# Layer normalisation without affine: two-pass statistics shared by three engines, rows normalised on GpSimd

## The chip, the cores and the metric

One NeuronCore of a Trainium2 chip runs the kernel. The metric is device time in microseconds (us), the median of several executions; the profile gives a span that is 1.7 to 2.5 us shorter. Engines are named as in the profile: DVE is VectorE, ACT is ScalarE, POOL is GpSimd, SP issues DMAs; ACTq and SPq are the instruction queues of ACT and SP. Where an instruction works on 8 or 1024 elements, that is per partition.

## The reference

```python
x = np.random.randn(32, 512, 1024).astype(np.float32)      # eps = 1e-5
mean = np.mean(x, axis=-1, keepdims=True)
var = np.var(x, axis=-1, keepdims=True)
return ((x - mean) / np.sqrt(var + eps)).astype(np.float32)
```

There are 16384 rows of 1024 numbers. A tile of K takes K rows on each of 128 partitions, so the whole is 128 rows a partition. 67.1 MB are read and 67.1 MB written.

## The kernel before

A ring of 48 rows a partition in SBUF holds six tiles of 8 rows. SP issues the loads, ACT the stores. DVE takes batch-norm statistics of each half row; ten small POOL operations make the mean and the squared sum of 8 rows at a time; ACT takes the root and normalises in place.

```python
TILES = (2, 2, 4) + (8,) * 14 + (4, 2, 2)
...
        for k in range(G):
            for s in range(NSUB):                       # NSUB = 2 halves of 512
                nc.vector.bn_stats(out=stats[:, k, s, :],
                                   in_=xs[:, k, s * BN_MAX : (s + 1) * BN_MAX])
...                                                     # ten small GpSimd operations: nmean, ss, nmr
        nc.scalar.activation(out=std[:, :G], in_=ss[:, :G], func=AF.Sqrt, bias=eps_t, scale=1.0 / D)
        nc.vector.reciprocal(out=rstd[:, :G], in_=std[:, :G])
...
        for k in range(G):
            nc.scalar.activation(out=xs[:, k, :], in_=xs[:, k, :], func=AF.Identity,
                                 bias=nmr[:, k : k + 1], scale=rstd[:, k : k + 1])
...
        for K, row, pos in place(TILES, RING):
            nc.sync.dma_start(out=ring[:, pos : pos + K, :], in_=rows_of(x2, row, K))
            group(...)
            nc.scalar.dma_start(out=rows_of(o2, row, K), in_=ring[:, pos : pos + K, :])
```

Of the kernel before, what the change touches and what calls it, by code (L numbers as in the profile page):

```python
# [1 line left out]

# [4 lines left out]


TILES = (2, 2, 4) + (8,) * 14 + (4, 2, 2)  # L10

RING = 48

GROUP = 8


def place(tiles, ring):

    plan, row, pos = [], 0, 0
    for K in tiles:  # L20
        if pos + K > ring:
            pos = 0
        plan.append((K, row, pos))
        row += K
        pos += K
    return plan


@with_exitstack
def kernel(  # L30
    ctx: ExitStack,
    tc: tile.TileContext,
    x: bass.AP,
    eps: bass.AP,
    out: bass.AP,
):
    nc = tc.nc
    P = nc.NUM_PARTITIONS
    eps_val = float(eps) if not isinstance(eps, bass.AP) else 1e-5

    x2 = x.flatten_outer_dims()
    o2 = out.flatten_outer_dims()
    N, D = x2.shape
    BN_MAX = nc.vector.BN_STATS_FMAX
    NSUB = D // BN_MAX
    assert sum(TILES) * P == N

    rings = ctx.enter_context(tc.tile_pool(name="rings", bufs=1))
    st = ctx.enter_context(tc.tile_pool(name="st", bufs=4))

    fdt = mybir.dt.float32
    AF = mybir.ActivationFunctionType
    ALU = mybir.AluOpType

    ring = rings.tile([P, RING, D], fdt)
    eps_t = rings.tile([P, 1], fdt)

    def rows_of(a, row, K):
        return a[row * P : (row + K) * P].rearrange("(p k) d -> p k d", p=P)

    def pool_sum(o, terms):
        G = terms.shape[1]
        half = st.tile([P, GROUP, 2], fdt, name="half")
        nc.gpsimd.tensor_tensor(  # L64
            out=half[:, :G], in0=terms[:, :, 0:2], in1=terms[:, :, 2:4], op=ALU.add
        )
        nc.gpsimd.tensor_tensor(  # L67
            out=o, in0=half[:, :G, 0], in1=half[:, :G, 1], op=ALU.add
        )

    def group(xs, G):
        stats = st.tile([P, GROUP, NSUB, 6], fdt, name="stats")
        for k in range(G):
            for s in range(NSUB):
                nc.vector.bn_stats(  # L75
                    out=stats[:, k, s, :],
                    in_=xs[:, k, s * BN_MAX : (s + 1) * BN_MAX],
                )

        H = 2 * NSUB  # L80
        parts = stats[:, :G].rearrange("p g s (h c) -> p g (s h) c", h=2)
        mean4, m2 = parts[:, :, :, 1], parts[:, :, :, 2]
        nmean = st.tile([P, GROUP], fdt, name="nmean")
        dev = st.tile([P, GROUP, H], fdt, name="dev")
        ss = st.tile([P, GROUP], fdt, name="ss")
        pool_sum(nmean[:, :G], mean4)
        nc.gpsimd.tensor_scalar(  # L87
            out=nmean[:, :G], in0=nmean[:, :G], scalar1=-1.0 / H, scalar2=None, op0=ALU.mult
        )
        nc.gpsimd.tensor_tensor(  # L90
            out=dev[:, :G],
            in0=mean4,
            in1=nmean[:, :G].unsqueeze(2).to_broadcast([P, G, H]),
            op=ALU.add,
        )
        nc.gpsimd.tensor_mul(out=dev[:, :G], in0=dev[:, :G], in1=dev[:, :G])  # L96
        nc.gpsimd.tensor_scalar(  # L97
            out=dev[:, :G], in0=dev[:, :G], scalar1=float(D // H), scalar2=None, op0=ALU.mult
        )
        nc.gpsimd.tensor_tensor(out=dev[:, :G], in0=dev[:, :G], in1=m2, op=ALU.add)  # L100
        pool_sum(ss[:, :G], dev[:, :G])
        std = st.tile([P, GROUP], fdt, name="std")
        nc.scalar.activation(  # L103
            out=std[:, :G], in_=ss[:, :G], func=AF.Sqrt, bias=eps_t, scale=1.0 / D
        )
        rstd = st.tile([P, GROUP], fdt, name="rstd")
        nc.vector.reciprocal(out=rstd[:, :G], in_=std[:, :G])  # L107
        nmr = st.tile([P, GROUP], fdt, name="nmr")
        nc.gpsimd.tensor_mul(out=nmr[:, :G], in0=nmean[:, :G], in1=rstd[:, :G])  # L109
        for k in range(G):  # L110
            nc.scalar.activation(  # L111
                out=xs[:, k, :],
                in_=xs[:, k, :],
                func=AF.Identity,
                bias=nmr[:, k : k + 1],
                scale=rstd[:, k : k + 1],
            )

    with tc.manual_schedule():
        nc.vector.memset(eps_t, eps_val)  # L120
        for K, row, pos in place(TILES, RING):
            nc.sync.dma_start(out=ring[:, pos : pos + K, :], in_=rows_of(x2, row, K))
            for g in range(0, K, GROUP):
                G = min(GROUP, K - g)
                group(ring[:, pos + g : pos + g + G, :], G)
            nc.scalar.dma_start(out=rows_of(o2, row, K), in_=ring[:, pos : pos + K, :])


# [1 line left out]
_INS = ['x', 'eps']  # L130
_OUTS = [((32, 512, 1024), 'float32')]

_NUMBERS = {'eps': 1e-05}


# [26 lines left out]
```

## Time and profile before

| | before |
|---|---|
| median time | 317.98 us (317.94 to 317.99) |
| span of the profile | 316.1 us |
| DVE, ACT, POOL busy | 157.1, 154.3, 45.1 us |
| load and store queue | 49.6% and 49.3% of 16 DMA engines |
| from one tile's statistics to the next | 19.4 us |

The two queues add up to 98.9% of what the DMA engines can do, and no engine is busy for more than half of the span. The lines that carry this stand in the prediction.

### The profile page before, as it was taken

The page shows a single profiled execution, that of the slowest core. Times are in us where ns is not written, and L with a number is a line of the kernel's source. Part 1 is how long each engine was busy: PE and PEld are TensorE (multiplying, and loading weights), DVE is VectorE, ACT ScalarE, POOL GpSimd, SP SyncE. Part 2 cuts the span into 40 slices and gives each one's busy share as a digit, 9 for nine tenths or more (in the row PEclk, how much of TensorE's full clock was granted, in tenths as well). Part 3 has the DMA queues.
Part 4 walks back from the last instruction along what each step waited for, and adds up shares of the span by engine and source line. Part 5 has one row for each costly group of instructions (what it writes and reads, how often), then busy time and mean ns, then how long its engine had stood idle before and what let it go on. Part 6 is the DMA issues. An engine that isn't in the chain of part 4 may idle for free.

```text
span 316.1 us, 794 instructions
## 1 busy us (share of the span) xinstructions
DVE 157.1 (50%) x277; ACT 154.3 (49%) x149; POOL 45.1 (14%) x204
## 2 busy tenths in 40 slices
DVE  2368596547092561916529074190652908363030
ACT  1336296692833809247091561900651956196321
POOL 0420202201102020020200202002020020221120
DMA  7999999999999999999999999999999999999996
GB/s 301 433 399 469 431 416 425 433 427 444 420 448 419 444 419 444 435 427 444 419 448 415 448 424 440 423 448 419 444 423 440 423 435 429 446 428 417 455 411 282
DMA packets 5766, 134.27 MB, mean 425 GB/s; under 512 B 640, under 2 KB 640, under 8 KB 640
## 3 DMA queue, kind: packets, MB, share of 16 engines
q1 hardware_dynamic: 2880, 67.11, 49.6%
q10 hardware_dynamic: 2880, 67.11, 49.3%
q14 instruction: 6, 0.05, 0.0%
HBM read 67.11 MB, written 67.11 MB: 425 GB/s over the span
## 4 chain that ended last, share of the span: by engine, by line
DMA 58%; DVE 17%; ACT 9%; POOL 6%; issue 3%; another core or an unknown queue 3%; ACTq 0%; POOLq 0%; DVEq 0%; SPq 0%
DMA ring<-in_x_dram 32%; DMA out_dram<-ring 27%; DVE stats L75 17%; ACT ring L111 8%; POOL half L64 1%; ACT std L103 1%; POOL dev L97 1%; POOL nmean L87 1%; POOL dev L100 1%; POOL dev L90 1%; POOL dev L96 1%; POOL nmean L67 1%; POOL ss L67 1%; DVE rstd L107 0%
## 5 line engine op out<-in xcount | busy, mean ns | idle before, releaser
L75 DVE BATCH_NORM_STATS2 stats<-ring 128x6 f32<-128x512 f32 x256 | 153.7, 678 | 71.2 <-DMA ring<-in_x_dram 71.2
L111 ACT ACTIVATE ring<-ring,nmr,rstd 128x1024 f32<-128x1024 f32 x128 | 147.0, 1227 | 10.8 <-POOL nmr L109 10.8
L103 ACT ACTIVATE std<-ss,eps_t 128x8 f32<-128x8 f32 (+2 forms) x20 | 6.0, 300 | 143.0 <-POOL ss L67 115.8
L107 DVE RECIPROCAL rstd<-std 128x8 f32<-128x8 f32 (+2 forms) x20 | 3.9, 193 | 77.3 <-ACT std L103 77.3
L64 POOL TENSOR_TENSOR half<-stats 128x16 f32<-128x16 f32 (+2 forms) x20 | 4.5, 226 | 221.0 <-DVE stats L75 221.0
L109 POOL TENSOR_TENSOR nmr<-nmean,rstd 128x8 f32<-128x8 f32 (+2 forms) x20 | 4.0, 202 | 27.2 <-DVE rstd L107 27.2
L97 POOL TENSOR_SCALAR dev<-dev 128x32 f32<-128x32 f32 (+2 forms) x20 | 5.6, 281 | 1.8
L100 POOL TENSOR_TENSOR dev<-dev,stats 128x32 f32<-128x32 f32 (+2 forms) x20 | 4.9, 243 | 1.7
L90 POOL TENSOR_TENSOR dev<-stats,nmean 128x32 f32<-128x32 f32 (+2 forms) x20 | 4.6, 231 | 1.7
L87 POOL TENSOR_SCALAR nmean<-nmean 128x8 f32<-128x8 f32 (+2 forms) x20 | 4.6, 228 | 1.8
L96 POOL TENSOR_TENSOR dev<-dev 128x32 f32<-128x32 f32 (+2 forms) x20 | 4.6, 228 | 1.6
L64 POOL TENSOR_TENSOR half<-dev 128x16 f32<-128x16 f32 (+2 forms) x20 | 4.2, 210 | 1.6
L67 POOL TENSOR_TENSOR nmean<-half 128x8 f32<-128x8 f32 (+2 forms) x20 | 4.0, 199 | 1.6
L67 POOL TENSOR_TENSOR ss<-half 128x8 f32<-128x8 f32 (+2 forms) x20 | 4.0, 199 | 1.6
L103 ACT ACT_TABLE_LOAD x1 | 1.3, 1283 | 0.9 <-DVE eps_t L120 0.9
L120 DVE MEMSET eps_t<- 128x1 f32 x1 | 0.1, 59 | 0.8 <-PEq L143 0.8
L143 POOL MEMSET const-float32-0.0<- 128x1 f32 x1 | 0.1, 98 | 0.2 <-issue 0.2
L143 POOL MEMSET const-uint8-127<- 128x1 uint8 x1 | 0.1, 102 | 0.0
L143 POOL MEMSET const-bfloat16-1.0<- 128x1 bf16 x1 | 0.1, 101 | 0.0
L143 POOL MEMSET const-float32-1.0<- 128x1 f32 x1 | 0.1, 98 | 0.0
## 6 DMA issues: line engine op xcount, KB each, us to landing
ring<-in_x_dram SPq DMA_DIRECT2D x14, 4096.0 KB, 47.3
out_dram<-ring ACTq DMA_DIRECT2D x14, 4096.0 KB, 40.7
ring<-in_x_dram SPq DMA_DIRECT2D x4, 1024.0 KB, 30.8
ring<-in_x_dram SPq DMA_DIRECT2D x2, 2048.0 KB, 27.2
out_dram<-ring ACTq DMA_DIRECT2D x4, 1024.0 KB, 16.7
out_dram<-ring ACTq DMA_DIRECT2D x2, 2048.0 KB, 24.5
```

Source lines behind the costliest of these rows:

```text
L64: nc.gpsimd.tensor_tensor(out=half[:, :G], in0=terms[:, :, 0:2], in1=terms[:, :, 2:4], op=ALU.add)
L67: nc.gpsimd.tensor_tensor(out=o, in0=half[:, :G, 0], in1=half[:, :G, 1], op=ALU.add)
L75: nc.vector.bn_stats(out=stats[:, k, s, :], in_=xs[:, k, s * BN_MAX : (s + 1) * BN_MAX],)
L87: nc.gpsimd.tensor_scalar(out=nmean[:, :G], in0=nmean[:, :G], scalar1=-1.0 / H, scalar2=None, op0=ALU.mult)
L90: nc.gpsimd.tensor_tensor(out=dev[:, :G], in0=mean4, in1=nmean[:, :G].unsqueeze(2).to_broadcast([P, G, H]), op=ALU.add,)
L96: nc.gpsimd.tensor_mul(out=dev[:, :G], in0=dev[:, :G], in1=dev[:, :G])
L97: nc.gpsimd.tensor_scalar(out=dev[:, :G], in0=dev[:, :G], scalar1=float(D // H), scalar2=None, op0=ALU.mult)
L100: nc.gpsimd.tensor_tensor(out=dev[:, :G], in0=dev[:, :G], in1=m2, op=ALU.add)
L103: nc.scalar.activation(out=std[:, :G], in_=ss[:, :G], func=AF.Sqrt, bias=eps_t, scale=1.0 / D)
L107: nc.vector.reciprocal(out=rstd[:, :G], in_=std[:, :G])
L109: nc.gpsimd.tensor_mul(out=nmr[:, :G], in0=nmean[:, :G], in1=rstd[:, :G])
L111: nc.scalar.activation(out=xs[:, k, :], in_=xs[:, k, :], func=AF.Identity, bias=nmr[:, k : k + 1], scale=rstd[:, k : k + 1],)
```

## The change

Its intent is to take the variance in two passes and to use the idle time of three engines. DVE sums the rows. POOL makes the negated mean. ACT squares the deviations, six of eight rows into PSUM and two with its own accumulator, and DVE sums those in PSUM. POOL, not ACT, normalises. Two tiles at the head and three at the tail keep batch-norm statistics (`bn`); of those, the last two are normalised by ACT, the others by POOL. Loads move to ACT's queue, stores to SP's; a load is issued two tiles after the tile whose rows it overwrites (`BEHIND = 2`). The pool of the batch-norm statistics has two buffers in place of four.

```diff
-TILES = (2, 2, 4) + (8,) * 14 + (4, 2, 2)
+TILES = (4, 4) + (8,) * 14 + (6, 2)
...
+    def two_pass(xs, K):
+        sums, ssq, std, rstd, nmean = map(small, ("sums", "ssq", "std", "rstd", "nmean"))
+        half = K // 2
+        for a in (0, half):
+            nc.vector.tensor_reduce(out=sums[:, a : a + half], in_=xs[:, a : a + half, :], axis=AX.X, op=ALU.add)
+        nc.gpsimd.tensor_scalar(
+            out=nmean[:, :K], in0=sums[:, :K], scalar1=-1.0 / D, scalar2=None, op0=ALU.mult
         )
+        def square(o, k, total=None):
+            nc.scalar.activation(out=o, in_=xs[:, k, :], func=AF.Square,
+                                 bias=nmean[:, k : k + 1], scale=1.0, accum_out=total)
+        def chunk(k):
+            sq = ps.tile([P, 2, D], fdt, name="sq")
+            for i in range(2):
+                square(sq[:, i, :], k + i)
+            nc.vector.tensor_reduce(out=ssq[:, k : k + 2], in_=sq, axis=AX.X, op=ALU.add)
+        chunk(0)
+        chunk(2)
+        for k in range(6, K):
+            square(junk, k, ssq[:, k : k + 1])
+        chunk(4)
...                                                     # root on ACT, reciprocal on DVE
+        for k in range(K):
+            nc.gpsimd.tensor_scalar(out=xs[:, k, :], in0=xs[:, k, :], scalar1=nmean[:, k : k + 1],
+                                    scalar2=rstd[:, k : k + 1], op0=ALU.add, op1=ALU.mult)
+    def bn(xs, K, on_scalar):
...                                                     # bn_stats and bn_aggr on DVE, root, reciprocal
+                nc.gpsimd.tensor_scalar(out=xs[:, k, :], in0=xs[:, k, :], scalar1=mv[:, k, 0:1],
+                                        scalar2=rstd[:, k : k + 1], op0=ALU.subtract, op1=ALU.mult)
...
+            if t < HEAD or left <= TAIL:                # HEAD = 2, TAIL = 3
+                bn(xs, K, on_scalar=left <= 2)
+            else:
+                two_pass(xs, K)
```

Both forms normalise a row on POOL with one instruction.

More of the change, by code (lines that the diff above doesn't have):

```diff
@@ L7 @@
 from concourse._compat import with_exitstack
-TILES = (2, 2, 4) + (8,) * 14 + (4, 2, 2)
+TILES = (4, 4) + (8,) * 14 + (6, 2)
 RING = 48
-GROUP = 8
-def place(tiles, ring):
-    plan, row, pos = [], 0, 0
-    for K in tiles:
-        if pos + K > ring:
-            pos = 0
-        plan.append((K, row, pos))
-        row += K
-        pos += K
-    return plan
+HEAD, TAIL = 2, 3
+BEHIND = 2
 @with_exitstack
@@ L48 @@
     rings = ctx.enter_context(tc.tile_pool(name="rings", bufs=1))
-    st = ctx.enter_context(tc.tile_pool(name="st", bufs=4))
+    st = ctx.enter_context(tc.tile_pool(name="st", bufs=2))
+    sm = ctx.enter_context(tc.tile_pool(name="sm", bufs=len(TILES)))
+    ps = ctx.enter_context(tc.tile_pool(name="ps", bufs=2, space=bass.MemoryType.PSUM))
     fdt = mybir.dt.float32
@@ L53, with small @@
     ALU = mybir.AluOpType
+    AX = mybir.AxisListType
+    GMAX = max(TILES)
     ring = rings.tile([P, RING, D], fdt)
+    junk = rings.tile([P, D], fdt)
     eps_t = rings.tile([P, 1], fdt)
+    def small(name):
+        return sm.tile([P, GMAX], fdt, name=name)
     def rows_of(a, row, K):
         return a[row * P : (row + K) * P].rearrange("(p k) d -> p k d", p=P)
-    def pool_sum(o, terms):
-        G = terms.shape[1]
-        half = st.tile([P, GROUP, 2], fdt, name="half")
-        nc.gpsimd.tensor_tensor(
-            out=half[:, :G], in0=terms[:, :, 0:2], in1=terms[:, :, 2:4], op=ALU.add
-        )
-        nc.gpsimd.tensor_tensor(
-            out=o, in0=half[:, :G, 0], in1=half[:, :G, 1], op=ALU.add
-        )
@@ L71, in group @@
-    def group(xs, G):
-        stats = st.tile([P, GROUP, NSUB, 6], fdt, name="stats")
-        for k in range(G):
+    def two_pass(xs, K):
+        sums, ssq, std, rstd, nmean = map(small, ("sums", "ssq", "std", "rstd", "nmean"))
+        half = K // 2
+        for a in (0, half):
+            nc.vector.tensor_reduce(
+                out=sums[:, a : a + half],
+                in_=xs[:, a : a + half, :],
+                axis=AX.X,
+                op=ALU.add,
+            )
+        nc.gpsimd.tensor_scalar(
+            out=nmean[:, :K], in0=sums[:, :K], scalar1=-1.0 / D, scalar2=None, op0=ALU.mult
+        )
+        def square(o, k, total=None):
+            nc.scalar.activation(
+                out=o,
+                in_=xs[:, k, :],
+                func=AF.Square,
+                bias=nmean[:, k : k + 1],
+                scale=1.0,
+                accum_out=total,
+            )
+        def chunk(k):
+            sq = ps.tile([P, 2, D], fdt, name="sq")
+            for i in range(2):
+                square(sq[:, i, :], k + i)
+            nc.vector.tensor_reduce(
+                out=ssq[:, k : k + 2], in_=sq, axis=AX.X, op=ALU.add
+            )
+        chunk(0)
[3 more added lines that the diff above has]
+        chunk(4)
+        nc.scalar.activation(
+            out=std[:, :K], in_=ssq[:, :K], func=AF.Sqrt, bias=eps_t, scale=1.0 / D
+        )
+        nc.vector.reciprocal(out=rstd[:, :K], in_=std[:, :K])
+        for k in range(K):
+            nc.gpsimd.tensor_scalar(
+                out=xs[:, k, :],
+                in0=xs[:, k, :],
+                scalar1=nmean[:, k : k + 1],
+                scalar2=rstd[:, k : k + 1],
+                op0=ALU.add,
+                op1=ALU.mult,
+            )
@@ L74, in group @@
+    def bn(xs, K, on_scalar):
+        stats = st.tile([P, GMAX, NSUB, 6], fdt, name="stats")
+        mv = st.tile([P, GMAX, 2], fdt, name="mv")
+        std, rstd = map(small, ("std", "rstd"))
+        for k in range(K):
             for s in range(NSUB):
@@ L78, in group @@
                 )
-        H = 2 * NSUB
-        parts = stats[:, :G].rearrange("p g s (h c) -> p g (s h) c", h=2)
-        mean4, m2 = parts[:, :, :, 1], parts[:, :, :, 2]
-        nmean = st.tile([P, GROUP], fdt, name="nmean")
-        dev = st.tile([P, GROUP, H], fdt, name="dev")
-        ss = st.tile([P, GROUP], fdt, name="ss")
-        pool_sum(nmean[:, :G], mean4)
-        nc.gpsimd.tensor_scalar(
-            out=nmean[:, :G], in0=nmean[:, :G], scalar1=-1.0 / H, scalar2=None, op0=ALU.mult
-        )
@@ L90, in group @@
-        nc.gpsimd.tensor_tensor(
-            out=dev[:, :G],
-            in0=mean4,
-            in1=nmean[:, :G].unsqueeze(2).to_broadcast([P, G, H]),
-            op=ALU.add,
-        )
-        nc.gpsimd.tensor_mul(out=dev[:, :G], in0=dev[:, :G], in1=dev[:, :G])
-        nc.gpsimd.tensor_scalar(
-            out=dev[:, :G], in0=dev[:, :G], scalar1=float(D // H), scalar2=None, op0=ALU.mult
-        )
-        nc.gpsimd.tensor_tensor(out=dev[:, :G], in0=dev[:, :G], in1=m2, op=ALU.add)
-        pool_sum(ss[:, :G], dev[:, :G])
@@ L102, in group @@
-        std = st.tile([P, GROUP], fdt, name="std")
-        nc.scalar.activation(
-            out=std[:, :G], in_=ss[:, :G], func=AF.Sqrt, bias=eps_t, scale=1.0 / D
-        )
-        rstd = st.tile([P, GROUP], fdt, name="rstd")
-        nc.vector.reciprocal(out=rstd[:, :G], in_=std[:, :G])
-        nmr = st.tile([P, GROUP], fdt, name="nmr")
-        nc.gpsimd.tensor_mul(out=nmr[:, :G], in0=nmean[:, :G], in1=rstd[:, :G])
-        for k in range(G):
-            nc.scalar.activation(
-                out=xs[:, k, :],
-                in_=xs[:, k, :],
-                func=AF.Identity,
-                bias=nmr[:, k : k + 1],
-                scale=rstd[:, k : k + 1],
-            )
@@ L119 @@
-    with tc.manual_schedule():
-        nc.vector.memset(eps_t, eps_val)
-        for K, row, pos in place(TILES, RING):
-            nc.sync.dma_start(out=ring[:, pos : pos + K, :], in_=rows_of(x2, row, K))
-            for g in range(0, K, GROUP):
-                G = min(GROUP, K - g)
-                group(ring[:, pos + g : pos + g + G, :], G)
-            nc.scalar.dma_start(out=rows_of(o2, row, K), in_=ring[:, pos : pos + K, :])
+            nc.vector.bn_aggr(out=mv[:, k, :], in_=stats[:, k, :, :])
@@ new lines, in bn @@
+        nc.scalar.activation(
+            out=std[:, :K], in_=mv[:, :K, 1], func=AF.Sqrt, bias=eps_t, scale=1.0
+        )
+        nc.vector.reciprocal(out=rstd[:, :K], in_=std[:, :K])
+        if on_scalar:
+            nmr = small("nmr")
+            nc.vector.scalar_tensor_tensor(
+                out=nmr[:, :K],
+                in0=mv[:, :K, 0],
+                scalar=-1.0,
+                in1=rstd[:, :K],
+                op0=ALU.mult,
+                op1=ALU.mult,
+            )
+        for k in range(K):
+            if on_scalar:
+                nc.scalar.activation(
+                    out=xs[:, k, :],
+                    in_=xs[:, k, :],
+                    func=AF.Identity,
+                    bias=nmr[:, k : k + 1],
+                    scale=rstd[:, k : k + 1],
+                )
+            else:
+                nc.gpsimd.tensor_scalar(
+                    out=xs[:, k, :],
+                    in0=xs[:, k, :],
+                    scalar1=mv[:, k, 0:1],
+                    scalar2=rstd[:, k : k + 1],
+                    op0=ALU.subtract,
+                    op1=ALU.mult,
+                )
@@ new lines, with load @@
+    plan, row, pos = [], 0, 0
+    for K in TILES:
+        if pos + K > RING:
+            pos = 0
+        plan.append((K, row, pos))
+        row += K
+        pos += K
+    after, owner = [], {}
+    for t, (K, row, pos) in enumerate(plan):
+        before = [owner[r] for r in range(pos, pos + K) if r in owner]
+        after.append(max(before) + BEHIND if before else -1)
+        owner.update((r, t) for r in range(pos, pos + K))
+    def load(done):
+        for t, (K, row, pos) in enumerate(plan):
+            if after[t] == done:
+                nc.scalar.dma_start(
+                    out=ring[:, pos : pos + K, :], in_=rows_of(x2, row, K)
+                )
@@ L130 @@
+    with tc.manual_schedule():
+        load(-1)
+        nc.gpsimd.memset(eps_t, eps_val)
+        for t, (K, row, pos) in enumerate(plan):
+            xs = ring[:, pos : pos + K, :]
+            left = len(TILES) - t
+            if t < HEAD or left <= TAIL:
+                bn(xs, K, on_scalar=left <= 2)
+            else:
+                two_pass(xs, K)
+            nc.sync.dma_start(out=rows_of(o2, row, K), in_=xs)
+            load(t)
 _INS = ['x', 'eps']
```

## The prediction

> **What bounds the kernel now.** I read the page of the profile from the top: the busy shares, the slices, the queues, then the costliest groups, and last the timeline of one tile in the middle.
>
> ```profile
> span 316.1 us, 794 instructions
> DVE 157.1 (50%) x277; ACT 154.3 (49%) x149; POOL 45.1 (14%) x204
> ...
> DMA  7999999999999999999999999999999999999996
> ...
> q1 hardware_dynamic: 2880, 67.11, 49.6%
> q10 hardware_dynamic: 2880, 67.11, 49.3%
> ```
>
> No compute engine is busy for more than half of the span, while the 16 DMA engines are full in 38 of 40 slices, and the load and store queues together take 98.9%. The table by stretches of time gives 435 GB/s for 60 to 120 us. A tile of 8 rows a partition is 4.194 MB in and the same out, so a tile costs 8.39 MB / 435 GB/s = 19.3 us of DMA. The whole is 134.2 MB / 435 GB/s = 308.6 us; the rest is the start and the end. The measured time is 1.9 us above the span.
>
> ```profile
> 138.92 9.16 ACT L111 ACTIVATE ring<-ring,nmr,rstd 128x1024 f32<-128x1024 f32 x8 [0.55 <-POOL nmr L109]
> 144.95 9.59 DVE L75 BATCH_NORM_STATS2 stats<-ring 128x6 f32<-128x512 f32 x16 [6.34 <-DMA ring<-in_x_dram]
> ...
> 157.42 0.30 ACT L103 ACTIVATE std<-ss,eps_t 128x8 f32<-128x8 f32 x1 [9.34 <-POOL ss L67]
> 157.75 0.20 DVE L107 RECIPROCAL rstd<-std 128x8 f32<-128x8 f32 x1 [3.22 <-ACT std L103]
> ...
> 164.31 1.29 DVE L75 BATCH_NORM_STATS2 stats<-ring 128x6 f32<-128x512 f32 x2 [6.35 <-DMA ring<-in_x_dram]
> ```
>
> From one tile's statistics to the next (144.95 to 164.31) pass 19.4 us, the DMA figure; VectorE waits 6.3 us in each for the load. So compute has slack of some 6 us a tile on the way from one tile to the next: a change that adds less to that way is free, one that adds more becomes the bound. Nothing can gain more than the 7 us between 308.6 and 316.1.
>
> **What the Trainium skill says.** "ScalarE: Activation LUTs", section What ACT_TABLE_LOAD costs: an ACTIVATE with a pointer bias takes 280 ns + 0.833 ns an element, each further pointer about 93 ns, and neighbours overlap by about 93 ns. For 1024 elements and two pointers that is 1226 ns, 1133 ns apart; the trace has 1227 ns, and (9.16 - 1.23) / 7 = 1.13 us apart. It agrees.
> "VectorE: DVE Perf Modes", section The perf-mode tier table: tensor_reduce runs at 1x for every operand, so one element a cycle of 0.96 GHz. The batch-norm instruction shows that rate here: (9.59 - 0.68) / 15 = 0.594 us for 512 elements, 0.533 us of it streaming and 0.06 us fixed.
> "GPSIMD Engine Reference", section Engine selection: a one-input operation is "roughly line-rate"; its section 3.1 gives 1.03 cycles an element for short bodies at 1.2 GHz. The trace does not clearly agree. The one tensor_scalar that it has in three sizes is
>
> ```profile
> L97 POOL TENSOR_SCALAR dev<-dev 128x32 f32<-128x32 f32 x14 | 4.2, 298 | 1.2
> L97 POOL TENSOR_SCALAR dev<-dev 128x8 f32<-128x8 f32 x4 | 0.9, 234 | 0.4
> ```
>
> which is (298 - 234) / 24 = 2.7 ns an element, three times line rate, on sizes where start-up may rule.
> "SBUF — State Buffer", section Who interferes with whom: DMA has ports of its own, and tensor_reduce never takes the port pair that VectorE shares with GpSimd. The full DMA row beside two half-busy engines agrees with the first; nothing here tests the second. I therefore add nothing for contention.
>
> **The change, part by part.** 13 tiles of 8 get the new statistics; two tiles of 4 at the head and three (8, 6, 2) at the tail keep batch-norm statistics, with the aggregate on VectorE. Gone are ten small GpSimd operations a tile, some 2.7 us of chain (154.62 to 157.3), which were hidden. The bytes are the same, and loads and stores only swap queues. What each new-style tile costs, as estimates from the rates above:
> VectorE, row sums: two reductions of 4096 elements, each 4.267 + 0.06 = 4.33, together 8.65 us.
> ScalarE, squares: one pointer, so 1.04 us apart; 7 x 1.04 + 1.13 = 8.4 us. The built order shows that the second of each pair waits on ScalarE's own semaphore, which costs the overlap: 4 x 0.12 = 0.5. Two also write an accumulator, for which I put 0.2 each, a guess. Sum 9.3 us.
> VectorE, square sums: three reductions of 2048 elements from PSUM, about 2.28 each; two lie beside ScalarE, the last one does not.
> Small steps: mean on GpSimd 0.23, square root 0.30, reciprocal 0.20, and six handovers of 0.02 to 0.08: 1.0 us.
> GpSimd, 8 rows of p each. At line rate p = 0.2 + 1024 x 1.03 / 1200 = 1.08 us, so 8.7 us; at 2.7 ns an element, 2.9 us and 23 us.
>
> Busy time stays below 19.3 us everywhere (VectorE 8.65 + 6.8 + 0.2 = 15.7, ScalarE 9.6, GpSimd 8.9 at line rate). Yet the order in which the instructions stand ties them into a ring. On GpSimd the mean of tile t+1 stands behind the 8 rows of tile t. On VectorE the row sums of t+1 stand behind the reciprocal of t. The squares of t+1 need that mean, and the reciprocal of t+1 needs all the squares. So no two tiles overlap, except that row sums of t+1 lie beside the rows of t on GpSimd. One turn of the ring is
>
> max(8.65, 8p) + 9.3 + 2.28 + 1.0 = 12.6 + 8.7 = 21.3 us
>
> against 19.3 us of DMA. I expect the ring to be the bound by 2 us a tile, with DMA no longer full.
>
> The sum. The first load of the old kernel took 4.95 us for 1.05 MB, 2.4 of that at 435 GB/s; the first of the new one has twice the bytes and lands near 8 us, the second near 13, the third (8 rows) near 26, since the first store shares the engines. Row sums end near 34.7, so the mean of the first new-style tile is at 34.8. Twelve turns of 21.3 and one more pass to the reciprocal (12.6) give 303. From there: 16 batch-norm instructions and 8 aggregates on VectorE (9.5 + 8 x 0.2 = 11.1), 0.6 of small steps, 8 rows on GpSimd (8.7) reach 323.4, where the store of the last full tile is issued; 4.19 MB take 9.65 us to 333. The stores of 6 and 2 rows queue behind it (ScalarE has written them by 331 and 333): 7.2 + 2.4 us, and about 1.5 us to land: 344, plus 1.9 is 346. I predict 345 us.
>
> **The rivals.** (1) DMA remains the bound and hides everything: 316 to 322 us. For it: the ring of 48 rows still holds six tiles, the loads of seven tiles are issued at once, and my 21.3 is only 10% above 19.3. With no fixed cost at all a turn is 8.53 + 6.83 + 2.13 = 17.5 us, so some 1.8 us of overhead would have to stay away out of 3.8, and the tail of 41 us after the last new-style reciprocal would remain. Against it: those overheads are measured ones.
> (2) GpSimd at the rate of its small operations, p = 2.9: a turn is 12.6 + 23 = 35.8 us, GpSimd alone is busy for 120 x 2.9 = 348 us, and the time is near 345 + 12 x 14.5 + 2 x 14.5 = 545 us. For it: the two lines above. Against it: the skill's statement, and the change itself, which gives GpSimd all of 120 rows while ScalarE keeps half of its time. At 1.75 us a row the time would be about 345 + 14 x 5.4 = 420. I give rates clearly above line rate a fifth.
> (3) The load issue, now in ScalarE's program behind the square root, blocks ScalarE until a store two tiles back has landed. That store is issued some 33 us before (two turns less 9.3), and with stores alone queued 4.19 MB need under 20 us even at half the rate; so it should not bind.
>
> **Range and chances.** Between a line-rate GpSimd with cheap waits (turn of 20.3, about 331 us) and 1.5 us a row (near 393) lies what I hold for 8 in 10: 328 to 400 us. Faster by over 2% would need under 311.6, next to the floor of 308.6: 0.01. Within 2% needs a turn at or below 19.4 and a short tail: 0.06. Slower: 0.93.
>
> **What would show it.** In the new profile the DMA row should have 8s and 9s with gaps, not 9 throughout; the chain that ended last should consist of VectorE sums, ScalarE squares and GpSimd rows, not DMA; the reciprocal should return every 21 us; the wide tensor_scalar should be near 1.1 us; the load issue on ScalarE should show little waiting for stores. I am wrong if turns of 19.4 us come with full DMA, or if the wide tensor_scalar is far from 1.1 us, which scales everything by 8p a turn.

## The result

The changed kernel takes 385.08 us (384.99 to 385.16, 4 runs) against 317.97 us for the kernel before in the same rounds. The ratio is 1.2111, with a 95% interval of 1.209 to 1.2132. "Slower" was right, and the time lies inside the stated range of 328 to 400 us, but the stated 345 us was an increase of 27 us and the measured one is 67.

From the page of the profile after: the span, the DMA row, the queues and the chain that ended last:

```profile
span 383.2 us, 595 instructions
...
DMA  8999999999899898999999999989898090720397
...
q10 hardware_dynamic: 2592, 67.11, 42.7%
q1 hardware_dynamic: 2592, 67.11, 41.9%
...
POOL 44%; ACT 27%; issue 13%; DVE 8%; DMA 2%; POOLq 1%; ACTq 0%
```

The bytes are the same, yet the two queues take only 42.7 + 41.9 = 84.6% of a longer span. DMA has almost left the chain, at 2%. Through the middle there are small gaps, and at the end whole empty slices.

The timeline of one turn, in the middle:

```profile
166.68 0.20 DVE L101 RECIPROCAL rstd<-std 128x8 f32<-128x8 f32 x1 [0.37 <-ACT std L98]
166.80 8.70 DVE L65 TENSOR_REDUCE sums<-ring 128x4 f32<-128x4096 f32 x2
166.99 9.42 POOL L103 TENSOR_SCALAR ring<-ring,nmean,rstd 128x1024 f32<-128x1024 f32 x8 [12.07 <-DVE rstd L101]
176.37 0.23 POOL L71 TENSOR_SCALAR nmean<-sums 128x8 f32<-128x8 f32 x1
176.64 4.45 ACT L76 ACTIVATE sq<-ring,nmean 128x1024 f32<-128x1024 f32 x4 [9.98 <-POOL nmean L71]
...
185.71 2.29 DVE L89 TENSOR_REDUCE ssq<-sq 128x2 f32<-128x2048 f32 x1 [2.29 <-ACT sq L76]
188.03 0.30 ACT L98 ACTIVATE std<-ssq,eps_t 128x8 f32<-128x8 f32 x1 [2.36 <-DVE ssq L89]
188.04 0.33 ACTq L175 DMA_DIRECT2D ring<-in_x_dram  x1
188.37 0.20 DVE L101 RECIPROCAL rstd<-std 128x8 f32<-128x8 f32 x1 [0.37 <-ACT std L98]
```

The reciprocal returns after 21.69 us. The pieces follow each other without slack. ACT waits 9.98 us for the mean, POOL 12.07 us for the reciprocal, and only the row sums of the next tile lie beside the rows of this one. The load is issued at once behind the root (188.04), so it waits for no store.

What I had not foreseen is in the groups of instructions (line, engine, operation, shapes and count; busy us and mean ns; idle time before):

```profile
L103 POOL TENSOR_SCALAR ring<-ring,nmean,rstd 128x1024 f32<-128x1024 f32 x104 | 122.4, 1194 | 156.9 <-DVE rstd L101 156.9
L147 POOL TENSOR_SCALAR ring<-ring,mv,rstd 128x1024 f32<-128x1024 f32 x16 | 60.2, 3780 | 17.7 <-DVE rstd L126 17.7
```

One row takes 1.19 us in the two-pass tiles and 3.78 us in the batch-norm tiles: same engine, same shape, same instruction name. And the timeline shows where the 16 slow ones stand, at both ends:

```profile
16.16 30.11 POOL L147 TENSOR_SCALAR ring<-ring,mv,rstd 128x1024 f32<-128x1024 f32 x8 [15.35 <-DVE rstd L126]
...
46.24 0.24 POOL L71 TENSOR_SCALAR nmean<-sums 128x8 f32<-128x8 f32 x1
...
330.51 30.13 POOL L147 TENSOR_SCALAR ring<-ring,mv,rstd 128x1024 f32<-128x1024 f32 x8 [2.32 <-DVE rstd L126]
```

At the head the first small mean stands in POOL's order behind 8 slow rows, until 46.24, though its row sums ended at 31.8. At the tail, 8 slow rows keep the store of the last full tile back until 360.6 us, and SP, which issues stores in order, holds the other two stores behind it. The last tile's statistics wait too: DVE stands still for 19.94 us until 360.68, when those rows end. The new aggregate needs the buffer from which the rows read the mean, and there are two. This probably costs little, as the last store would have queued behind the other two in any case; no run tests it alone.

The theory after this reading has two parts. **Ring** (here a closed chain of waits, not the buffer `ring` in SBUF; going round it once is a turn): mean, squares, last reduction, root, reciprocal and rows of a tile are one chain that the order of instructions closes from tile to tile. **Form:** the subtracting POOL instruction is slow by its operations. The rivals are that the slow rows come from where their operand lies (the mean is every second element of the aggregate tile), from contention or their place; and that the turn is set by some engine's throughput, or by DMA slowed by the engines.

### The profile page after: what moved, and what is told of

It is laid out like the page before. It is cut to its first block, busy times and chain, and to the rows that moved or that the text cites. A ratio compares the mean times of both kernels' runs of the same rounds, so it can differ in the third digit from the quotient of the medians.

```text
span 383.2 us, 595 instructions
## 1 busy us (share of the span) xinstructions
DVE 237.0 (62%) x157; ACT 131.8 (34%) x157; POOL 185.6 (48%) x138
## 3 DMA queue, kind: packets, MB, share of 16 engines
q10 hardware_dynamic: 2592, 67.11, 42.7%
q1 hardware_dynamic: 2592, 67.11, 41.9%
## 4 chain that ended last, share of the span: by engine, by line
POOL 44%; ACT 27%; issue 13%; DVE 8%; DMA 2%; POOLq 1%; ACTq 0%
POOL ring L103 29%; ACT sq L76 19%; POOL ring L147 14%; ACT junk L76 7%; DVE ssq L89 7%; DMA ring<-in_x_dram 2%; POOLq L221 1%; ACT std L98 1%; POOL nmean L71 1%; DVE rstd L101 1%; ACT ring L139 0%; DVE stats L118 0%; ACTq L221 0%; DVE mv L122 0%; ACT std L123 0%
## 5 line engine op out<-in xcount | busy, mean ns | idle before, releaser
L103 POOL TENSOR_SCALAR ring<-ring,nmean,rstd 128x1024 f32<-128x1024 f32 x104 | 122.4, 1194 | 156.9 <-DVE rstd L101 156.9
L89 DVE TENSOR_REDUCE ssq<-sq 128x2 f32<-128x2048 f32 x39 | 88.1, 2288 | 87.9 <-ACT sq L76 87.9
L76 ACT ACTIVATE sq<-ring,nmean 128x1024 f32<-128x1024 f32 x78 | 85.8, 1111 | 145.7 <-POOL nmean L71 144.4
L65 DVE TENSOR_REDUCE sums<-ring 128x4 f32<-128x4096 f32 x26 | 113.2, 4393 | 0.9 <-DMA ring<-in_x_dram 0.9
L147 POOL TENSOR_SCALAR ring<-ring,mv,rstd 128x1024 f32<-128x1024 f32 x16 | 60.2, 3780 | 17.7 <-DVE rstd L126 17.7
L118 DVE BATCH_NORM_STATS2 stats<-ring 128x6 f32<-128x512 f32 x48 | 29.7, 661 | 8.5 <-DMA ring<-in_x_dram 8.5
L76 ACT ACTIVATE junk<-ring,nmean 128x1024 f32<-128x1024 f32 x26 | 29.6, 1140 | 0.4
L122 DVE BATCH_NORM_AGGREGATE mv<-stats 128x2 f32<-128x12 f32 x24 | 5.0, 209 | 20.7 <-POOL ring L147 19.9
L139 ACT ACTIVATE ring<-ring,nmr,rstd 128x1024 f32<-128x1024 f32 x8 | 9.3, 1228 | 0.9 <-DVE nmr L129 0.9
L76 ACT ACTIVATION_READ_ACCUMULATOR junk<-ring,nmean 128x1 f32 x26 | 4.9, 187 | 0.0
L181 POOL MEMSET eps_t<- 128x1 f32 x1 | 0.1, 98 | 0.3 <-POOLq L207 0.3
```

What stands on the lines that cost most here:

```text
L65: nc.vector.tensor_reduce(out=sums[:, a : a + half], in_=xs[:, a : a + half, :], axis=AX.X, op=ALU.add,)
L76: nc.scalar.activation(out=o, in_=xs[:, k, :], func=AF.Square, bias=nmean[:, k : k + 1], scale=1.0, accum_out=total,)
L89: nc.vector.tensor_reduce(out=ssq[:, k : k + 2], in_=sq, axis=AX.X, op=ALU.add)
L103: nc.gpsimd.tensor_scalar(out=xs[:, k, :], in0=xs[:, k, :], scalar1=nmean[:, k : k + 1], scalar2=rstd[:, k : k + 1], op0=ALU.add, op1=ALU. ...
L118: nc.vector.bn_stats(out=stats[:, k, s, :], in_=xs[:, k, s * BN_MAX : (s + 1) * BN_MAX],)
L122: nc.vector.bn_aggr(out=mv[:, k, :], in_=stats[:, k, :, :])
```

## The experiments

Each edit is to the changed kernel. All runs gave correct results. The runs of the kernel before beside them had medians of 318.1 to 318.5 us.

### Adding in place of subtracting (e1)

```diff
+        if not on_scalar:
+            nm = small("nm")
+            nc.vector.tensor_scalar(out=nm[:, :K], in0=mv[:, :K, 0], scalar1=-1.0, scalar2=None, op0=ALU.mult)
-                    scalar1=mv[:, k, 0:1],
+                    scalar1=nm[:, k : k + 1],
-                    op0=ALU.subtract,
+                    op0=ALU.add,
```

> The batch-norm tiles' 8 + 8 GpSimd rows add a negated mean from a small tile of its own instead of subtracting the mean that lies in the aggregate. Theory A (the subtract is what is slow on GpSimd): a row falls from 3.78 to 1.19 us, the first mean moves from 46.2 to about 32.1 us (then the row sums, ending at 31.8, bind), the tail loses 8 x 2.6 = 20.7 us: 385 - 14 - 21 = 350 us. Rival B (the strided operand of the aggregate is slow): the same here, told apart by e3. Rival C (GpSimd rows are slow there through contention with VectorE or through their place): rows stay at 3.8 us and the time at 385. The ring's turn stays at 21.7 us in all.

Measured: 350.3 us, ratio 1.1003 (1.0986 to 1.1019).

```profile
L152 POOL TENSOR_SCALAR ring<-ring,nm,rstd 128x1024 f32<-128x1024 f32 x16 | 18.9, 1200 | 19.2 <-DVE nm L129 19.2
```

The rows of the batch-norm tiles fell to 1.20 us; the first mean came at 31.84 us; the reciprocals of the last two two-pass tiles stand at 282.68 and 304.40, 21.72 us apart. So 34.8 of the 67 us are the 16 slow rows, and contention and place are out. The edit changed both the operation and the operand; e3 separates them.

### Subtracting everywhere (e2)

The 13 two-pass tiles get a positive mean in a small contiguous tile, and subtract it.

```diff
+        mean = small("mean")
+        nc.gpsimd.tensor_scalar(out=mean[:, :K], in0=sums[:, :K], scalar1=1.0 / D, scalar2=None, op0=ALU.mult)
-                scalar1=nmean[:, k : k + 1],
+                scalar1=mean[:, k : k + 1],
-                op0=ALU.add,
+                op0=ALU.subtract,
```

> The 13 two-pass tiles subtract a positive mean (one more small GpSimd step a tile) instead of adding a negated one; that mean lies in a small contiguous tile. Theory A: rows there rise from 1.19 to 3.78 us, the turn from 21.7 to 12.3 + 30.2 + 0.5 = 43 us, the time to about 385 + 13 x 21.2 = 660 us. Rival B (strided operand) and C: rows stay near 1.2 us, 385 + 13 x 0.3 = 389 us.

Measured once: 653.45 us; the rows took 3.78 us.

```profile
L108 POOL TENSOR_SCALAR ring<-ring,mean,rstd 128x1024 f32<-128x1024 f32 x104 | 391.8, 3781 | 155.5 <-issue 155.5
```

The operand is contiguous here, so its layout is not the cause. The ring passed the cost on in full: the time rose by 268 us, and the 104 rows by 391.8 - 122.4 = 269 us.

### Which forms of a row are quick (e3, e8)

The 8 rows of the two head tiles take different instructions, each on a line of its own (and again the 8 slow rows of the tail). Only durations are read. In e3:

```python
f == 0: ts(row, row, mv[:, k, 0:1], r, subtract, mult)      # as in the change
f == 1: ts(row, row, mean[:, k],    r, subtract, mult)      # contiguous mean
f == 2: ts(row, row, mvn[:, k, 0:1], r, add, mult)          # strided, negated
f == 3: ts(row, row, nm[:, k],      r, add, mult)
f == 4: ts(row, row, r, nmr[:, k], mult, add)
f == 5: ts(row, row, r, mr[:, k],  mult, subtract)
f == 6: ts(row, row, mean[:, k], None, subtract); ts(row, row, r, None, mult)
f == 7: ts(row, row, 1.0, None, mult); ts(row, row, nm[:, k], None, add); tensor_tensor(row, row, r broadcast, mult)
```

> The two head tiles' 8 rows take eight forms of the same normalisation, each on its own line; a count of durations, not of the whole time. Theory A: every form with a subtract in either place takes about 3.8 us (subtract then multiply with strided and with contiguous mean, multiply then subtract), all forms of add and multiply about 1.2 us, and the single subtract is slower than the single add. Rival B: both forms with the strided mean are slow, both with the contiguous one fast. The single multiply by a constant tells whether the 2.7 ns an element of the small operations in the kernel before hold at 1024 elements: then it takes about 2.9 us, else about 1.1.

The groups, with the lines in the order of `f`: L168, L170, L172, L174, L176, L178, L180 and L181, L183 to L185; L176 and L185, not shown, took 1.20 and 1.89 us.

```profile
L168 POOL TENSOR_SCALAR ring<-ring,mv,rstd 128x1024 f32<-128x1024 f32 x2 | 7.6, 3804 | 17.9 <-DVE rstd L126 15.6 <-DVE mean L133 2.3
L178 POOL TENSOR_SCALAR ring<-ring,rstd,mr 128x1024 f32<-128x1024 f32 x2 | 7.6, 3793 | 0.0
L170 POOL TENSOR_SCALAR ring<-ring,mean,rstd 128x1024 f32<-128x1024 f32 x2 | 7.6, 3778 | 0.0
L180 POOL TENSOR_SCALAR ring<-ring,mean 128x1024 f32<-128x1024 f32 x2 | 5.7, 2850 | 0.0
L184 POOL TENSOR_SCALAR ring<-ring,nm 128x1024 f32<-128x1024 f32 x2 | 5.7, 2850 | 0.2
L181 POOL TENSOR_SCALAR ring<-ring,rstd 128x1024 f32<-128x1024 f32 x2 | 5.7, 2846 | 0.2
L183 POOL TENSOR_SCALAR ring<-ring 128x1024 f32<-128x1024 f32 x2 | 5.5, 2771 | 0.0
...
L174 POOL TENSOR_SCALAR ring<-ring,nm,rstd 128x1024 f32<-128x1024 f32 x2 | 2.4, 1196 | 0.0
L172 POOL TENSOR_SCALAR ring<-ring,mvn,rstd 128x1024 f32<-128x1024 f32 x2 | 2.4, 1196 | 0.0
```

The strided operand costs nothing (L172 beside L174), and a subtract in either place gives 3.8 us. But part of the expectation fell: a single subtract is no slower than a single add or multiply. All three take 2.85 us (L180, L184, L181), so a single multiply costs more than twice as much as an add and a multiply together. The subtract is not slow in itself; certain pairs are quick. The second set asks which.

```python
f == 0: ts(row, row, nm, 0.0, add, add); ts(row, row, r, 0.0, mult, add)    # L158, L170
f == 1: ts(row, row, 1.0, 0.0, mult, add)                                   # L160, then a row of add, mult
f == 2: ts(row, row, 1.0, 0.0, mult, subtract)                              # L162, likewise
f == 3: ts(row, row, 1.0, 1.0, mult, mult)                                  # L164
f == 4: ts(row, row, -100.0, 100.0, max, min)                               # L166
f == 5: tensor_copy(row, row)                                               # L168
f == 6: ts(row, row, nm, 1.0, add, mult); ts(row, row, r, None, mult)       # L172, L173
```

> More forms of a 128 x 1024 GpSimd tensor_scalar in the head tiles, one a line; a count of durations. If the quick 1.2 us belongs to a pair of operations made of add and multiply only: add then add, multiply then add, multiply then multiply with constants 1.2 us each; a pair with a subtract, and max then min, 3.8 us. If it belongs to mixed pairs with pointer operands only: the pairs with constants are slow too, 2.8 us or more. A plain copy beside them: no expectation.

```profile
L158 POOL TENSOR_SCALAR ring<-ring,nm 128x1024 f32<-128x1024 f32 x2 | 7.4, 3724 | 17.8 <-DVE nm L129 17.8
L162 POOL TENSOR_SCALAR ring<-ring 128x1024 f32<-128x1024 f32 x2 | 7.3, 3652 | 0.0
...
L170 POOL TENSOR_SCALAR ring<-ring,rstd 128x1024 f32<-128x1024 f32 x2 | 2.2, 1116 | 0.2
...
L160 POOL TENSOR_SCALAR ring<-ring 128x1024 f32<-128x1024 f32 x2 | 2.1, 1044 | 0.0
L164 POOL TENSOR_SCALAR ring<-ring 128x1024 f32<-128x1024 f32 x2 | 2.1, 1044 | 0.0
L168 POOL COPY ring<-ring 128x1024 f32<-128x1024 f32 x2 | 2.1, 1036 | 0.0
```

Quick are multiply-add and multiply-multiply with constants, at 1.04 us as quick as a copy, and multiply-add and add-multiply with per-row operands: 1.11 to 1.12 us with one (L170, and L172, not shown), 1.19 to 1.20 with two. Multiply-multiply was not run with per-row operands, nor add-multiply with constants alone. Add-add, which the expectation had among the quick ones, takes 3.72 us; max-min takes 3.63 (L166), and the pairs with a subtract 3.65 to 3.80. A multiply with a neutral second operation, an added zero, takes 1.12 us against 2.85 for the bare multiply. Which instructions inside GpSimd make this so, no run here shows.

The whole times, 381.53 us (e3) and 378.12 us (e8), are those of one execution each and play no part.

### The squares without PSUM (e4)

```diff
-        chunk(0)
-        chunk(2)
-        for k in range(6, K):
+        for k in range(K):
             square(junk, k, ssq[:, k : k + 1])
-        chunk(4)
```

> All 8 squares of a tile use ScalarE's accumulator; no PSUM, no square sums on VectorE. Ring theory (statistics and rows of a tile are one chain, so the last 2.3 us reduction lies on it): the turn falls by 2.3 and rises by 6 x 0.13 us of accumulator reads, to about 20.1 us; 13 x 1.5 = 20 us less, 365 us. Rival (VectorE's square sums are hidden beside ScalarE, ScalarE is what counts): the turn rises by 0.8 us, 395 us. Rival (GpSimd's or DMA's throughput binds): 385 us.

Measured: 369.18 us, ratio 1.1594 (1.1575 to 1.1613). ACT's eight squares now take 10.2 us (1.27 each with the read of the accumulator), 1.1 us more than before, yet a turn takes 20.5 us (reciprocals at 159.75 and 180.25). The last reduction, 2.3 us with its handover, did lie on the path. Compared with the change, 15.9 us are gained by giving ACT more work and DVE less. The direction and most of the size are the ring's; I had the accumulator read at 0.13 us where it added 0.19.

### Row sums and mean one tile ahead (e5)

The reductions and the mean of tile t+1 are emitted before the squares of tile t. Every instruction is the same; only the order on DVE and POOL differs.

```diff
-    def two_pass(xs, K):
+    def means(xs, K):                       # the two row sums and the negated mean; returns nmean
...
+    def two_pass(xs, K, nmean, then):
+        ahead = then()                      # means() of the next two-pass tile
         chunk(0)
         chunk(2)
```

> The two row sums and the mean of tile t+1 are emitted before the squares of tile t; nothing else changes, the subtracting rows stay. Ring theory: a turn is no longer rows, squares, last reduction in line; VectorE's 8.7 + 3 x 2.29 + about 0.8 = 16.4 us is left, below the 19.3 us of DMA, so the middle runs at the DMA's rate and the time falls by at least 12 x 2.3 = 28 us to 357; DMA has been full up to 60 us, so by bytes it may be 340. The 30 us of subtracting rows at the end stay. Rival (a turn of 21.7 is some engine's throughput, or DMA slowed by the engines): 385 us, no change.

Measured: 333.62 us, ratio 1.0493 (1.0472 to 1.0515), 51.5 us less than the change. The reciprocals, from the timeline of DVE:

```profile
90.14 0.20 DVE L106 RECIPROCAL rstd<-std 128x8 f32<-128x8 f32 x1 [0.37 <-ACT std L103]
106.14 0.20 DVE L106 RECIPROCAL rstd<-std 128x8 f32<-128x8 f32 x1 [0.37 <-ACT std L103]
...
177.65 0.20 DVE L106 RECIPROCAL rstd<-std 128x8 f32<-128x8 f32 x1 [0.37 <-ACT std L103]
197.01 0.20 DVE L106 RECIPROCAL rstd<-std 128x8 f32<-128x8 f32 x1 [0.37 <-ACT std L103]
```

The first turns take 16.0 us, VectorE's own (16.4 expected; it is busy for 58.4 of the 60 us from 60 to 120), and the later ones 19.4 us, the DMA's. So the turn of 21.7 us was neither an engine's throughput nor DMA slowed by the engines; it was the order. The gain is above 28 us because the loads had run ahead of the compute: until it has caught up with them, a turn saves 5.7 us and not 2.3. The 30 us of subtracting rows at the end stay, and the empty slice of the DMA row lies there.

### The tail on ScalarE (e6)

```diff
-                bn(xs, K, on_scalar=left <= 2)
+                bn(xs, K, on_scalar=left <= 3)
```

> Only the 8 rows of the third last tile go from GpSimd to ScalarE (9.2 us in place of 30.1); the head keeps its subtracting rows. If the slow rows at the tail lie wholly on the path: 385 - 21 = 364 us, so that 14 of e1_add's 35 us are the head's. If the stores that queue up behind were the tail's bound: above 375 us.

Measured once: 363.69 us. ACT normalised the third last tile in 9.16 us. The tail's slow rows are on the path with all of their 21 us, and 14 us of e1's 35 are the head's.

### Both repairs (e7)

The edits of e1 and e5 together.

> e5_ahead and e1_add together. If the ring and the slow subtract are the whole of the loss, DMA is the bound again: 318 us, between 314 and 322, GB/s near 430 in the middle, turns of 19.4 us. If something else of the change costs time (PSUM, three engines at once slowing DMA, loads from ScalarE's queue), it stays above 325 us.

Measured: 317.44 us (317.26 to 317.54, 4 runs) against 318.13 us in the same rounds; ratio 0.9975 (0.996 to 0.999). That is a gain of a quarter of a per cent on the kernel before, within 2% and so the same, but the quickest version that I ran. The DMA row of its page, and a turn:

```profile
DMA  7999999999999999999999999999999999999996
...
164.52 0.33 ACTq L186 DMA_DIRECT2D ring<-in_x_dram  x1
164.96 4.45 ACT L80 ACTIVATE sq<-ring,nmean 128x1024 f32<-128x1024 f32 x4 [7.82 <-DMA out_dram<-ring]
...
176.69 0.20 DVE L106 RECIPROCAL rstd<-std 128x8 f32<-128x8 f32 x1 [0.37 <-ACT std L103]
...
196.08 0.20 DVE L106 RECIPROCAL rstd<-std 128x8 f32<-128x8 f32 x1 [0.37 <-ACT std L103]
```

The DMA row is the one of the kernel before, digit for digit. A turn is 19.39 us, though DVE is busy for 75% of the span, and PSUM, three engines and the loads in ACT's queue are all as in the change. The load at 164.52 is issued, and the squares behind it start, only when a store has landed: ACT stood for 7.82 us, and for 44.5 us in six such waits of this run. This is the third rival of the prediction, come true where it costs nothing that shows: DMA is full and the turn is the DMA's. With both repairs the change's extra work is hidden again, and DMA bounds both kernels, so there is little left to gain.

### The mean on VectorE, and on ScalarE (e9, e10)

e9 moves only the mean of the two-pass tiles, without any change of order between tiles; e10 puts it on ScalarE.

```diff
-        nc.gpsimd.tensor_scalar(out=nmean[:, :K], in0=sums[:, :K], scalar1=-1.0 / D, scalar2=None, op0=ALU.mult)
+        nc.vector.tensor_scalar(out=nmean[:, :K], in0=sums[:, :K], scalar1=-1.0 / D, scalar2=None, op0=ALU.mult)   # e9
+        nc.scalar.activation(out=nmean[:, :K], in_=sums[:, :K], func=AF.Copy, scale=-1.0 / D)                      # e10
```

> Only the small mean of the two-pass tiles goes from GpSimd, where it stands behind the 8 rows of the tile before, to VectorE behind the row sums. Ring theory with two branches from the reciprocal on (row sums 8.7 us on VectorE, rows 9.4 us on GpSimd, of which the longer counts): the branch over GpSimd is cut, the one over VectorE stays, so a turn falls only by about 0.9 us to 20.8, the time by 13 x 0.9 to 373. If the place of the mean behind the rows were the whole cause, as a reader of the GpSimd order alone might think: turns at the DMA's 19.4 us, some 356 us. The slow subtract of the tail is left in both.

Measured: 370.53 us, ratio 1.1646 (1.1626 to 1.1665). Near the 373 expected, but not for the reason given. The turn is 21.58 us (174.33 to 195.91), 0.1 less and not 0.9. The gain is at the head, where the first squares start at 32.5 us and not at 46.5, since the mean no longer stands behind the slow rows; I had left that out. And the mean itself:

```profile
174.70 9.42 POOL L103 TENSOR_SCALAR ring<-ring,nmean,rstd 128x1024 f32<-128x1024 f32 x8 [11.06 <-ACT std L98]
183.19 0.95 DVE L71 TENSOR_SCALAR nmean<-sums 128x8 f32<-128x8 f32 x1
```

An operation on 8 elements takes 0.95 us, and ends at 184.14, when the rows on POOL end (184.12). In 11 of the 13 tiles it ends so. In one it took 0.18 us, beside the rows too, and the turn that ended with that tile was 20.81 us (153.52 to 174.33), the expected one. So the wait of the mean is what kept the turn long. It reads as VectorE being held by the rows on GpSimd, and e10 tests it; why one tile escaped, no run shows.

> As e9_mean_vector, but the small mean is taken on ScalarE[...]. In e9 the mean on VectorE stood at 0.9 us and ended when GpSimd's 8 rows ended in tile after tile, against 0.18 us free. If that is a hold by the rows on GpSimd, as opposed to a slow operation, the ScalarE mean takes about 0.25 us here, the branch over the row sums alone is left, a turn falls from 21.58 to about 20.9 and the time by 12 x 0.7 = 8 us to 362. If the turn is bound by the rows in another way (rows of t+1 or squares waiting on rows of t), it stays at 21.6 and 370 us.

Measured: 360.53 us, ratio 1.1332 (1.1313 to 1.1351). The mean takes 0.21 us on ACT in all 13 tiles, beside the same rows on POOL, and does not wait for them:

```profile
177.67 0.21 ACT L71 ACTIVATE nmean<-sums 128x8 f32<-128x8 f32 x1 [8.89 <-DVE sums L65]
```

The turn is 20.84 us (reciprocals at 168.82 and 189.66), as expected of the branch over the row sums alone. The head gains as in e9 (first squares at 32.0), and the rest of the 24.6 us is the shorter turn. So two branches of nearly equal length leave the reciprocal, rows and mean on POOL (9.42 + 0.23) and row sums on DVE (8.70); cutting one leaves the other, and only e5, which cuts both, reaches the DMA's 19.4.

## Why the prediction was right or wrong

**The bound: right.** DMA stopped being the bound, and the ring took its place. The turn was put at 21.3 us and measured 21.68; e4, e5 and e10 each moved it as the ring says (e4 to 20.5 us where 20.1 was expected). Of the signs that the prediction named, the gaps in the DMA row, the return of the reciprocal, and the loads that do not wait came true. VectorE's row sums are not in the chain, since the rows beside them took longer.

**The terms of the turn: right within a tenth.** Row sums 8.70 us (8.65 expected), squares 9.04 from the first start to the last end, 46.52 to 55.56 (9.3), last reduction 2.29 (2.28), the mean 0.23, root 0.30, reciprocal 0.20. Rows of the two-pass tiles took 9.42 us (8.7): 1.19 us for p = 1.08; the pairs with constants took 1.04 in e8, so the two per-row operands make up some 0.15. Over 12 turns, 0.38 us more a turn make 4.6 us.

**The step that failed: "GpSimd, 8 rows of p each", with one p for all 120 rows.** The change has two forms of that instruction. The estimate of 1.08 us came close for 104 of the rows (1.19), and the other 16 took 3.78. At the head, the first mean came at 46.2 us, not 34.8; at the tail, the 8 rows took 30.1 us, not 8.7. Together with the 4.6 us above, 11.4 + 21.4 + 4.6 = 37.4 of the 40 us between 345 and 385 are the slow rows at the head, those at the tail and the longer turn; most of the rest is in the last stores. e1, where all rows have the quick form, took 350.3 us against the predicted 345. Part of that nearness is luck: its first mean came 3 us early (31.84 against 34.8), which took back 3 of the 5 us that the longer turns cost. The prediction had named a wide tensor_scalar far from 1.1 us as one sign of being wrong, and for 16 rows it came true.

**The evidence that was set aside.** The prediction showed two lines of the kernel before, 2.7 ns an element for a multiply by a constant, and weighed them as a rival for all rows or none. They were right for what they measured: the same multiply on 1024 elements took 2.77 us in e3, 2.7 ns an element with its fixed part spread over them. The error was to let one number of GpSimd's tensor_scalar stand for another: the lines were of a single operation, the rows are pairs, and the two kinds of pair in the diff differ by a factor of three.

**The other rivals.** DMA hiding everything was wrong for the change, and is what e7 gives, with another order of instructions and the quick form of row. Loads blocked on ACT did not bind, as argued. Contention was put at nothing, and nothing in the change's trace needs it; it showed in e9. Two sums among the rivals are slightly off and change nothing: 345 + 12 x 14.5 + 2 x 14.5 is 548, not 545, and from 21.3 to 19.3 us some 2.0 us of overhead would have had to stay away, not 1.8.

**Head and tail: right but for the rows.** The third load was put near 26 us and landed before 23.1. That the slow rows held back the stores is not why: in e1, whose first store was issued at 20.94, it had landed by 23.0 too. The store simply came too late to share much of the engines with this load. The last stores took 22.6 us from the issue of the first (360.6) to the end (383.2), against 20.6.

## What to carry to other kernels

Busy shares say nothing about a chain that the program order closes: write down what stands in front of what on each engine, from one tile to the next, and add up one turn. Emitting one stage a tile ahead, with not an instruction changed, was worth 51 us here. And when an instruction's cost is taken from another line of the profile, check that the operations are the same ones, not only the opcode and the shape; on GpSimd, write a normalisation of fp32 rows like these as add-multiply or multiply-add, and a lone multiply with a neutral second operation.

## What the Trainium skill lacked or had wrong

- "GPSIMD Engine Reference", section Engine selection, says that a one-input operation is "roughly line-rate". On 128 x 1024 fp32 this held for copy (1.04 us), multiply-add, multiply-multiply (1.04 us with constants) and add-multiply (1.11 to 1.20 with one or two per-row operands). It did not for a single add, subtract or multiply (2.77 to 2.85 us), nor for add-add, max-min and pairs with a subtract (3.63 to 3.80 us). No page that I read has this difference.
- "SBUF — State Buffer", section Who interferes with whom, says that a VectorE tensor_scalar can take the port pair that it shares with GpSimd, held for one instruction. The runs agree that such an operation waits, even on 8 elements: in ten of 13 tiles the mean took 0.87 to 0.95 us and ended with the rows on GpSimd (e9), against 0.12 us for a like one while GpSimd was idle (e1, at 316.25). No wait shows for the mean on ScalarE (e10) or for tensor_reduce (4.37 to 4.42 us each, with rows beside it or not). They do not agree on one instruction as the length: once the wait was 2.67 us, over back-to-back rows of 1.18 us until the last of them ended; beside the slow rows of 3.78 us the mean took 0.59 us and ended in the middle of a row (31.24 to 35.00); and once it took 0.18 us beside quick rows.
- No page gives what the accumulator output of an ACTIVATE costs: a separate read of 0.19 us behind each, and squares 1.27 us apart in place of about 1.1 (e4).
